# An MLP's up product as seven block products (Strassen) in three of its four groups, with the weight sums on GpSimd

## The chip, the cores and the metric

The kernel runs on one core of one Trainium2 chip. The metric is the device time of one launch in microseconds (us). A core has a matrix engine (TensorE, PE in the profile, with its weight loads as PEld), a vector engine (VectorE, DVE), a scalar engine (ScalarE, ACT), GpSimd (POOL) and SyncE (SP), which issues DMAs. Each engine runs its own instructions in order and waits for the others at semaphores.

## The reference

A trunk of two layers over 512 positions of 1024 channels, float32. Layer 0 mixes tokens with a gated DeltaNet, layer 1 with a Conformer convolution module. Each layer then cross-attends to a memory of 256 positions and applies the MLP that is changed here:

```python
def rms_norm(x, g):
    y = x * lax.rsqrt(jnp.mean(x * x, axis=-1, keepdims=True) + RMS_EPS)
    return y * g

def sq_relu_mlp(h, w_up, w_down):          # w_up (1024, 4096), w_down (4096, 1024)
    return jnp.square(jax.nn.relu(h @ w_up)) @ w_down

# in both layers
h = h + sq_relu_mlp(rms_norm(h, mlp_norm[layer]), mlp_w_up[layer], mlp_w_down[layer])
```

At the end stands a last RMS norm.

## The kernel before

Every float32 operand of a matmul is split into a high part (rounded to fp32r) and the low rest, and a product is three matmuls: high x high, low x high and high x low (`mm3`, L292 to L294). Activations lie with channels on partitions and 512 tokens along the row. `Norm.parts` makes the split of the MLP's input times its gain, without the root: `xs[k]` for k = 0 to 7. The factor 1/rms per token is computed by `Norm.stat` (a matmul with ones, a root, a reciprocal) and spread over partitions as `norm.rb`.

Weights come in a single stream, written out ahead in `order`, `loads` and `need`. `wload` issues one DMA of 128x1024 floats (512 KB) on SP's queue into a `raw` tile (six buffers); where blocks of the down product's weights must be added, `more` issues further DMAs on GpSimd's queue that add in flight, in part into `t` tiles (three buffers, tag `fs`). `wsplit` makes of a raw tile the high part `wh` on ScalarE (L251, a cast) and the low part `wl` on VectorE (L71, a subtraction); of `wh` and `wl` there are three buffers each. `wnext` hands out the next pair, issues loads some way ahead and splits up to three ahead. Which instruction stands where on its engine is settled when the program is built, by a scheduler with its own estimates; the text's order is not binding on it.

`mlp7(layer, norm, hres, ...)` works in four groups of 1024 of the 4096 hidden channels. In each group the up product makes eight tiles of 128 hidden channels x 512 tokens: eight times 24 matmuls with the weights as the stationary operand (128x128) and 512 tokens moving. `up_ev` takes a tile from PSUM: relu and the factor `norm.rb` in one VectorE step (`rl`, L77), the square on ScalarE (`u2`, L1100). `early` and `late` form differences and sums of halves of these tiles and split them into `ah`, `al`, `sh`, `sl`.

The down product `dn7` is already a Strassen scheme in Winograd's form: seven products of 512 x 256 x 512 instead of eight, in the order of `ORDER7` (in the last group `LAST7`), each on two units of weights and 24 matmuls of 512 columns. `into` adds a product to its accumulator `acc` on VectorE. Tokens 0 to 255 and 256 to 511 are the two row blocks. In the last group the weights' sums are made differently, and the results go on: in layer 0 through transposes (`outs`), in layer 1 through `final` to the output. In layer 1 `turn` puts the residual, transposed, into the accumulators during the first group.

## Time and profile before

| what | before |
|---|---|
| time, median of 3 runs | 1466.11 us (1464.77 to 1466.46) |
| profiled execution | 1465.14 us |
| its span, first to last instruction | 1463.4 us |
| granted TensorE clock | 0.998 |
| busy: PE, DVE, ACT, POOL | 1452.9, 1065.2, 771.2, 266.8 us |
| up product, 1536 matmuls of 512 columns | 351.3 us |
| down product, 1344 matmuls of 512 columns | 306.7 us |
| data moved by DMA | 201.82 MB, 138 GB/s on average |

Busy times are sums over one execution. Matmuls overlap in the pipeline, so a row's mean duration (about 390 ns at 512 columns) is longer than the spacing of their starts. In grouped rows stand: line, engine, operation, output tile <- inputs, shapes, count | busy us, mean ns of one | idle us of the engine just before them, and who ended it. A line can be that of a helper: L71 is every `tensor_tensor`, L77 every `scalar_tensor_tensor`.

### The profile page before, as it was taken

What the parts mean: (1) busy time and instruction counts of PE and PEld (TensorE: products, weight loads), DVE (VectorE), ACT (ScalarE), POOL (GpSimd) and SP (SyncE); (2) the same over time, 40 slices, a digit from 0 to 9 for tenths busy, and PEclk for the clock granted to TensorE, in tenths of its full rate; (3) what the DMA queues carried; (4) which work ended last, traced back from release to release, by engine and by line L of the source; (5) the groups of instructions that cost most, each with busy time, mean ns of one, the idle gap of its engine ahead of it and who ended that gap; (6) DMA issues with size and microseconds to landing.
All of it is one profiled execution on the core that took longest, in us unless ns stands there. A gap on an engine that the chain in (4) does not pass through costs nothing.

```text
span 1463.4 us, 19623 instructions
## 1 busy us (share of the span) xinstructions
PE 1452.9 (99%) x7298; PEld 1225.5 (84%) x7298; DVE 1065.2 (73%) x1615; ACT 771.2 (53%) x1326; POOL 266.8 (18%) x289
## 2 busy tenths in 40 slices
PE   9999999999999999999999999999999999999997
PEld 7888889988888888888888889988888888888886
DVE  6879889867646766767679899985555776767677
ACT  7766865655434464435355655564444544434354
POOL 1411310103113000010000486402113010000100
PEclk9999999999999999999999999999999999999999
DMA  8232124442213666584766624533214566575853
GB/s 283 84 115 73 59 87 158 132 143 87 72 44 108 166 165 179 140 199 136 202 159 215 185 82 162 179 129 100 72 51 127 139 169 177 135 210 131 229 144 87
DMA packets 62735, 201.82 MB, mean 138 GB/s; under 512 B 7728, under 2 KB 10032, under 8 KB 62640
## 3 DMA queue, kind: packets, MB, share of 16 engines
q1 hardware_dynamic: 52416, 164.39, 33.4%
q0 software_dynamic: 9792, 35.66, 14.3%
q8 instruction: 57, 0.93, 0.3%
q10 hardware_dynamic: 432, 0.52, 0.1%
q14 instruction: 38, 0.31, 0.1%
HBM read 197.66 MB, written 2.10 MB: 136 GB/s over the span
## 4 chain that ended last, share of the span: by engine, by line
PE 94%; DVE 3%; ACT 2%; DMA 1%; issue 0%; POOL 0%; SPq 0%; POOLq 0%; DVEq 0%
PE up L292 8%; PE up L294 8%; PE up L293 8%; PE dn L1130 6%; PE dn L1128 6%; PE dn L1129 6%; PE pw L294 3%; PE pw L292 3%; PE pw L293 3%; PE h L292 3%; PE h L293 3%; PE h L294 3%; PE xo L293 2%; PE xo L294 2%; PE q L292 2%; PE q L293 2%
## 5 line engine op out<-in xcount | busy, mean ns | idle before, releaser
L251 ACT CAST wh<-raw 128x1024 fp32r<-128x1024 f32 x259 | 271.6, 1051 | 358.7 <-issue 97.0
L71 DVE TENSOR_TENSOR wl<-raw,wh 128x1024 fp32r<-128x1024 f32 (+1 forms) x250 | 304.2, 1219 | 104.3 <-ACT wh L251 98.5
L292 PE MATMUL up<-xh,wh 128*128 128x512 f32 x512 | 199.7, 390 | 0.0
L294 PE MATMUL up<-xh,wl 128*128 128x512 f32 x512 | 199.3, 389 | 0.0
L293 PE MATMUL up<-xl,wh 128*128 128x512 f32 x512 | 199.2, 389 | 0.0
L294 PEld LDWEIGHTS up<-xh,wl 128*128 128x128 f32 x512 | 96.1, 188 | 20.1
L293 PEld LDWEIGHTS up<-xl,wh 128*128 128x128 f32 x512 | 96.2, 188 | 19.8
L292 PEld LDWEIGHTS up<-xh,wh 128*128 128x128 f32 x512 | 96.1, 188 | 19.7
L239 POOL DMA_DIRECT2D t<-w_dn x48 | 42.1, 915 | 354.2 <-DVE wl L71 239.0
L1128 PE MATMUL dn<-wh,ah 128*128 128x512 f32 x256 | 99.8, 390 | 0.0
L1130 PE MATMUL dn<-wl,ah 128*128 128x512 f32 x256 | 99.6, 389 | 0.0
L1129 PE MATMUL dn<-wh,al 128*128 128x512 f32 x256 | 99.6, 389 | 0.0
L77 DVE SCALAR_TENSOR_TENSOR rl<-up,rb 128x512 f32<-128x512 f32 x64 | 44.1, 690 | 58.4 <-PE up L294 58.4
L1358 DVE SCALAR_TENSOR_TENSOR ca<-x,prm,ca 128x512 f32<-128x512 f32 x112 | 82.3, 752 | 3.9 <-ACT ca L1355 1.5
L251 ACT CAST wh<-t 128x1024 fp32r<-128x1024 f32 x44 | 46.4, 1055 | 55.8 <-PE dn L1129 43.7
L71 DVE TENSOR_TENSOR wl<-t,wh 128x1024 fp32r<-128x1024 f32 x44 | 53.7, 1223 | 29.5 <-ACT wh L251 29.3
L292 PE MATMUL h<-xh,wh 128*128 128x512 f32 x184 | 73.7, 400 | 0.0
L71 POOL TENSOR_TENSOR sq<-sq,sq 128x512 f32<-128x512 f32 x28 | 45.4, 1621 | 148.3 <-ACT sq L385 134.2
L294 PE MATMUL h<-xh,wl 128*128 128x512 f32 x184 | 71.9, 391 | 0.0
L293 PE MATMUL h<-xl,wh 128*128 128x512 f32 x184 | 71.7, 390 | 0.0
L71 DVE TENSOR_TENSOR acc<-acc,dn 128x512 f32<-128x512 f32 x100 | 67.3, 682 | 1.2
L71 DVE TENSOR_TENSOR al<-u,ah 128x512 fp32r<-128x512 f32 x64 | 44.1, 688 | 21.4 <-ACT ah L331 21.4
(385 smaller groups left out, 3560.1 us busy)
## 6 DMA issues: line engine op xcount, KB each, us to landing
raw<-w_dn SPq DMA_DIRECT2D x68, 512.0 KB, 3.7
raw<-w_up SPq DMA_DIRECT2D x64, 512.0 KB, 4.3
t<-w_dn POOLq DMA_DIRECT2D x48, 512.0 KB, 6.0
raw<-w_pw SPq DMA_DIRECT2D x24, 512.0 KB, 3.7
raw<-w_dn POOLq DMA_DIRECT2D x20, 512.0 KB, 5.9
raw<-w_k SPq DMA_DIRECT2D x16, 512.0 KB, 3.6
raw<-w_vv SPq DMA_DIRECT2D x16, 512.0 KB, 4.1
t<-w_dn SPq DMA_DIRECT2D x16, 512.0 KB, 3.5
```

The source lines that it names most:

```text
L71: r = e.tensor_tensor(out=o, in0=a, in1=b, op=op)
L77: return dve.scalar_tensor_tensor(out=o, in0=a, scalar=s, in1=b, op0=op0, op1=op1)
L239: nc.gpsimd.dma_start(out=t, in_=a, accum_op=ALU.add)
L251: ins = [act.copy(h, raw)]
L292: pe.matmul(ps, wh, xh, start=first, stop=False)
L293: pe.matmul(ps, wh, xl, start=False, stop=False)
L294: pe.matmul(ps, wl, xh, start=False, stop=last)
L1128: pe.matmul(ps, xh, w[0][:, s], start=opens and k == 0, stop=False, skip_group_check=True)
L1129: pe.matmul(ps, xl, w[0][:, s], start=False, stop=False, skip_group_check=True)
L1130: pe.matmul(ps, xh, w[1][:, s], start=False, stop=k == 3, skip_group_check=True)
L1358: first["tap"] = dve.scalar_tensor_tensor(out=a, in0=src, scalar=w, in1=a, op0=ALU.mult, op1=ALU.add)
```

## The change

In groups two to four (g = 1 to 3; `PLAIN = 1`) of both layers the up product is also made of seven block products. A group has two halves `sg` of 512 hidden channels. In each half the 1024 x 512 weight block is cut into four blocks of 512 channels x 256 hidden channels, named 11, 12, 21, 22, and the input into halves by channels and by tokens. A block product is 24 matmuls with 256 tokens moving (L1329 to L1331 of the new file), into half of a PSUM bank per 128 hidden channels. Of the seven, products 0 and 2 go to one bank, 4 and 6 to another.

The four raw weight blocks are loaded as they are (four DMAs instead of four whole units, the same bytes). The sums T3 = 22 + 12, T1 = 12 + 11, T2 = 11 + T3 and T4 = 21 + T2 are made in place on GpSimd, in this order, once the plain blocks 11, 22 and 21 are split; each sum is then split as a unit of its own: seven casts and seven subtractions for a half instead of four. The sums on the input's side (`x_sums`) are made once a layer, during the second half of group one.

`fast` combines the products on VectorE (`uP`, `uQ`, `uW`), applies relu and square on ScalarE in two steps, forms the down product's operands (R3, R2, S1, S4) from whole blocks and splits all seven. Group one keeps the plain product, with the loops turned so that the first four input tiles are used up first.

The factor 1/rms is no longer applied to the hidden channels. relu(s x)^2 = s^2 relu(x)^2 for positive s, so the accumulators are multiplied by 1/rms^2 per token: `Norm.columns` computes rms^2, its reciprocal and the negative as columns by token; at the last group the accumulators so far are scaled on ScalarE, and the last group's products are scaled as they are added (`into`); `turn` multiplies the residual by rms^2 beforehand. The split of the sum of squares, the root, its reciprocal over 512 columns and the `rl` step are gone in the MLP.

In the built program the products of a first half stand on PE in the order of `UP7`. In a second half the third of them (12 by 21) stands behind the first matmuls of product 5, so that the order is 0, 1, 3, 4, 5 in part, 2, 5, 6, and some matmuls of the down product stand ahead of product 6's. The cast of T1 stands on ScalarE ahead of the copy of product 0 (`uP`).

```diff
+    def block_up(layer, g, sg, b):
+        a = int(b[0]) - 1
+        return w_up[layer, g * 4 + sg * 2 + int(b[1]) - 1][:, a * 1024:(a + 1) * 1024]
+
     def plan_mlp7(layer):
         for g in range(4):
-            for i in range(4):
-                plan(("up", layer, g * 4 + i), w_up[layer, g * 4 + i])
+            if g < PLAIN:
+                for i in range(4):
+                    plan(("up", layer, g * 4 + i), w_up[layer, g * 4 + i])
+            else:
+                for sg in range(2):
+                    n = len(loads)
+                    for b in UPLOAD:
+                        loads.append([block_up(layer, g, sg, b)])
+                    for u in range(7):
+                        order.append((("ups", layer, g, sg), u))
+                        need.append(n + (UPLOAD.index(UP7[u][1]) if u < 3 else 3))
...
+        if kind == "ups" and hf == 2:
+            t = TU
+            t["12"] = ws["raw"].pop(need[u] - 1)
+            for x, y in (("22", "12"), ("12", "11"), ("11", "22"), ("21", "11")):
+                tt(pool, t[x], t[x], t[y], ALU.add)
...
+    def combos_up(u, hf):
+        name = UP7[hf][1]
+        if hf < 3:
+            TU[name] = ws["raw"].pop(need[u])
+            return TU[name]
+        return TU[{"T1": "12", "T2": "11", "T4": "21", "T3": "22"}[name]]
...
+        def columns(self):
+            ps = psum("ssq")
+            for c in range(4):
+                pe.matmul(ps[:, c:c + 1], self.acc[:, c * P:(c + 1) * P], ones[:, 0:1], start=True, stop=True)
+            self.ms, self.r2, self.r2n = [keepc(4, s + str(self.cols)) for s in ("ms", "r2", "r2n")]
+            ts(dve, self.ms, ps[:, 0:4], 1.0 / 1024, ALU.mult, EPS, ALU.add)
+            dve.reciprocal(self.r2, self.ms)
+            ts(dve, self.r2n, self.r2, -1.0, ALU.mult)
...
-            act.copy(a, ps)
+            act.activation(a, ps, AF.Copy, scale=norm.ms[:, 2 * n + c:2 * n + c + 1])
...
-        def up_ev(ps):
-            t = slot(s="rl")
-            stt(t, ps, 0.0, norm.rb, ALU.max, ALU.mult)
-            u = slot(s="u2")
-            act.activation(u, t, AF.Square)
-            return u
+        def relu2(x, o):
+            act.activation(o, x, AF.Relu)
+            act.activation(o, o, AF.Square)
+            return o
...
+                elif g == 3 and key != ("p",):
+                    col = slice(2 * key[0] + c, 2 * key[0] + c + 1)
+                    dve.scalar_tensor_tensor(out=acc[k], in0=ps, scalar=(norm.r2 if op == ALU.add else norm.r2n)[:, col],
+                                             in1=acc[k], op0=ALU.mult, op1=ALU.add)
...
+        X = {"11": [[t[:, 0:256] for t in xs[k]] for k in range(4)],
+             "12": [[t[:, 0:256] for t in xs[4 + k]] for k in range(4)],
+             "22": [[t[:, 256:512] for t in xs[4 + k]] for k in range(4)], "R2": [], "S1": [], "R3": [], "S4": []}
+
+        def x_sums(k):
+            a, b = slot(s="xa"), slot(s="xb")
+            ga, gb = pc(norm.g, k), pc(norm.g, 4 + k)
+            tt(dve, b[:, 0:256], hres[k][:, 256:512], hres[k][:, 0:256], ALU.subtract)
+            act.activation(b[:, 0:256], b[:, 0:256], AF.Copy, scale=ga)
+            stt(a[:, 0:256], hres[4 + k][:, 256:512], gb, b[:, 0:256], ALU.mult, ALU.subtract)
+            stt(a[:, 256:512], hres[k][:, 0:256], ga, a[:, 0:256], ALU.mult, ALU.subtract)
+            stt(b[:, 256:512], hres[4 + k][:, 0:256], gb, a[:, 0:256], ALU.mult, ALU.subtract)
+            for t, names in ((a, ("R2", "S1")), (b, ("R3", "S4"))):
+                for name, p in zip(names, pair(split(t, "x"))):
+                    X[name].append(p)
+
+        def plain(g, sg, side):
+            us = []
+            for b in range(2):
+                pss = [psum("up") for _ in range(2)]
+                for a in range(2):
+                    w = wnext(("up", layer, g * 4 + sg * 2 + b), a)
+                    for j in range(2):
+                        for k in range(4):
+                            c = slice(k * 256 + j * P, k * 256 + j * P + P)
+                            mm3(pss[j], (w[0][:, c], w[1][:, c]), xs[4 * a + k], a == k == 0, a == 1 and k == 3)
+                            if (g, sg, b, a, j, k) == (0, 0, 0, 1, 0, 1):
+                                norm.columns()
+                    side(4 * sg + 2 * b + a)
+                us.append([relu2(ps, slot(s="u2")) for ps in pss])
+                for j in range(2):
+                    if b:
+                        late(ops[2 * sg + j], us[0][j], us[1][j])
+                    else:
+                        early(ops[2 * sg + j], us[0][j])
+
+        def fast(g, sg):
+            bank = {}
+
+            def product(u):
+                left, right, key, opens = UP7[u]
+                w = wnext(("ups", layer, g, sg), u)
+                if opens:
+                    bank[key] = psum("up")
+                for j in range(2):
+                    o = bank[key][:, j * 256:j * 256 + 256]
+                    for k in range(4):
+                        c = slice(k * 256 + j * P, k * 256 + j * P + P)
+                        xh, xl = X[left][k]
+                        pe.matmul(o, w[0][:, c], xh, start=opens and j == k == 0, stop=False, skip_group_check=True)
+                        pe.matmul(o, w[0][:, c], xl, start=False, stop=False, skip_group_check=True)
+                        pe.matmul(o, w[1][:, c], xh, start=False, stop=k == 3, skip_group_check=True)
+                return bank[key]
+
+            def give(name, x):
+                hl = split(x, "a")
+                for j in range(2):
+                    ops[2 * sg + j][name] = [t[:, j * 256:j * 256 + 256] for t in hl]

+            p, q, w, x11 = slot(s="uP"), slot(s="uQ"), slot(s="uW"), slot(s="u11")
+            act.copy(p, product(0))
+            f = product(1)
+            give("11", relu2(product(2), x11))
+            tt(dve, q, product(3), p, ALU.subtract)
+            tt(dve, w, product(4), q, ALU.add)
+            tt(dve, w, w, f, ALU.add)
+            give("12", relu2(w, w))
+            tt(dve, p, product(5), p, ALU.add)
+            b = product(6)
+            tt(dve, q, q, b, ALU.add)
+            tt(dve, p, p, b, ALU.subtract)
+            x22, x21 = relu2(q, q), relu2(p, p)
+            give("22", x22)
+            tt(dve, x21, x21, x11, ALU.subtract)
+            give("R3", x21)
+            tt(dve, x21, x22, x21, ALU.subtract)
+            give("R2", x21)
+            tt(dve, x11, x11, x21, ALU.subtract)
+            give("S1", x11)
+            tt(dve, w, w, x21, ALU.subtract)
+            give("S4", w)
...
+        def side(i):
+            if layer == 1:
+                if i:
+                    turn(i - 1)
+                if i == 7:
+                    turn(7)
+            if i > 3:
+                x_sums(i - 4)
...
+            if g == 3:
+                for n, m, c in [k for k in acc if len(k) == 3]:
+                    act.activation(acc[n, m, c], acc[n, m, c], AF.Copy, scale=norm.r2[:, 2 * n + c:2 * n + c + 1])
+            for sg in range(2):
+                if g < PLAIN:
+                    plain(g, sg, side if g == 0 else lambda i: None)
+                else:
+                    fast(g, sg)
...
+PLAIN = 1
+UPLOAD = ["11", "22", "12", "21"]
+UP7 = [("11", "11", "a", True), ("S4", "22", "f", True), ("12", "21", "a", False), ("S1", "T1", "c", True),
+       ("R2", "T2", "b", True), ("22", "T4", "e", True), ("R3", "T3", "b", False)]
```

More of the change, by code (lines that the diff above doesn't have):

```diff
@@ L246, in wsplit @@
         (kind, i, *j), hf = order[u]
-        raw = combos7(i, j[0], hf) if kind == "dn7" else ws["raw"].pop(need[u])
+        if kind == "dn7":
+            raw = combos7(i, j[0], hf)
+        elif kind == "ups":
+            raw = combos_up(u, hf)
+        else:
+            raw = ws["raw"].pop(need[u])
         h = wp.tile([P, 1024], F32R, tag="wh", name=nm("wh"), bufs=NW)
@@ L266, in wnext @@
         assert order[i] == (key, hf), (order[i], key, hf)
-        while ws["load"] <= need[min(i + NRAW + 1 + 2 * (order[i][0][0] in ("up", "dn7")), len(order) - 1)]:
+        while ws["load"] <= need[min(i + NRAW + 1 + 2 * (order[i][0][0] in ("up", "ups", "dn7")), len(order) - 1)]:
             wload()
@@ L272, in wnext @@
         return ws["hl"].pop(i)
+    TU = {}
+    def combos_up(u, hf):
[4 more added lines that the diff above has]
+        return TU[{"T1": "12", "T2": "11", "T4": "21", "T3": "22"}[name]]
     T7 = {}
@@ L368, in tile_trunk, with __init__ @@
     class Norm:
-        def __init__(self, gname):
-            self.g, self.acc, self.xs, self.n, self.side = gname, None, [], 0, None
+        def __init__(self, gname, cols=None):
+            self.g, self.acc, self.xs, self.n, self.side, self.cols = gname, None, [], 0, None, cols
         def add(self, t, h):
@@ L398, in square @@
                     tt(dve, self.acc, self.acc, self.side, ALU.add)
-                self.hl = split(self.acc, "sq")
+                if self.cols is None:
+                    self.hl = split(self.acc, "sq")
+        def columns(self):
[6 more added lines that the diff above has]
+            ts(dve, self.r2n, self.r2, -1.0, ALU.mult)
         def stat(self):
@@ L1234, in final @@
                 nc.sync.dma_start(out=yT[rows, gs], in_=y)
-        for g in range(4):
-            ops, us = [{} for _ in range(4)], []
-            for i in range(8):
-                w = wnext(("up", layer, g * 4 + i // 2), i % 2)
-                ps = psum("up")
-                proj(w, xs, ps, inside={1: norm.stat} if (g, i) == (0, 1) else None)
-                first.append(ps)
-                if (g, i) == (0, 0):
-                    continue
-                while first:
-                    us.append(up_ev(first.pop(0)))
-                    if len(us) % 2:
-                        early(ops[len(us) // 2], us[-1])
-                    else:
-                        late(ops[len(us) // 2 - 1], us[-2], us[-1])
-                if (layer, g) == (1, 0) and i > 1:
-                    turn(i - 2)
-            if (layer, g) == (1, 0):
-                turn(6)
-                turn(7)
+        X = {"11": [[t[:, 0:256] for t in xs[k]] for k in range(4)],
+             "12": [[t[:, 0:256] for t in xs[4 + k]] for k in range(4)],
+             "22": [[t[:, 256:512] for t in xs[4 + k]] for k in range(4)], "R2": [], "S1": [], "R3": [], "S4": []}
@@ new lines, in side @@
+        def side(i):
[6 more added lines that the diff above has]
+                x_sums(i - 4)
+        for g in range(4):
+            ops = [{} for _ in range(4)]
+            if g == 3:
[4 more added lines that the diff above has]
+                    plain(g, sg, side if g == 0 else lambda i: None)
+                else:
+                    fast(g, sg)
@@ L1687, in tile_trunk @@
         do_ev(m, do_mm(1, m))
-    n2 = Norm("mlp_norm0")
+    n2 = Norm("mlp_norm0", 0)
     h = xattn(0, n1, h, n2)
@@ L1693, in tile_trunk @@
     h = conformer(n3, h, n4, rest)
-    n5 = Norm("mlp_norm1")
+    n5 = Norm("mlp_norm1", 1)
     h = xattn(1, n4, h, n5)
@@ L1824, in _layout @@
     r["w_o"] = np.stack([_pack_a(np, i["xa_w_o"][j]) for j in range(2)])
-    halves = [8 * g + m for g in range(4) for m in (0, 4, 1, 5, 2, 6, 3, 7)]
-    r["w_up"] = np.stack([_pack_a(np, i["mlp_w_up"][j], halves) for j in range(2)])
+    r["w_up"] = f(np.stack(i["mlp_w_up"][:2]).reshape(2, 2, 4, 128, 4, 2, 2, 256).transpose(0, 4, 6, 5, 3, 1, 2, 7)
+                  .reshape(2, 16, 128, 2048))
     r["w_dn"] = np.stack([np.concatenate([_pack_b(np, i["mlp_w_down"][j][g * 1024:(g + 1) * 1024]) for g in range(4)]) for j in range(2)])
```

## The prediction

> **What bounds the kernel now.** I read the page's first block and chain, then PE's waits, then windows over one group of the MLP, then the timeline for the spacing of matmuls, last the grouped lines of the other engines.

> ```profile
> span 1463.4 us, 19623 instructions
> PE 1452.9 (99%) x7298; PEld 1225.5 (84%) x7298; DVE 1065.2 (73%) x1615; ACT 771.2 (53%) x1326; POOL 266.8 (18%) x289
> ...
> PE 94%; DVE 3%; ACT 2%; DMA 1%; issue 0%; POOL 0%; SPq 0%; POOLq 0%; DVEq 0%
> ```

> ```profile
> PE warm L130 <- POOL ones L127: 1.2, 1, 1.2
> PE h L1558 <- ACT xh L378: 1.0, 1, 1.0
> PE pw L294 <- POOL wl L71: 0.2, 1, 0.2
> PE dn L1130 <- DVE wl L71: 0.2, 1, 0.2
> ```

> TensorE is busy for 99% of the span and is 94% of the chain; its listed waits come to 2.6 us. So matmul time taken away is time won, as long as the other engines still deliver on time.

> ```profile
> core 0: us, PE busy (x) PEld busy (x) DVE busy (x) ACT busy (x) POOL busy (x), PEclk, DMA share, GB/s
> 555.50:599.00 43.50, 43.50 (x193) 36.05 (x192) 26.93 (x41) 19.45 (x29) 1.76 (x2) 1.00 0.58 158
> 599.00:637.10 38.10, 38.10 (x169) 31.54 (x168) 28.24 (x34) 16.76 (x19) 5.22 (x6) 1.00 0.70 178
> ```

> These are the second group of layer 0: its up product (192 matmuls, 43.5 us) and its down product (168 matmuls, 38.1 us). PE has no gap in either, and DVE is free for 16.6 and 9.9 us.

> **PE's side of the change.** A half group (96 matmuls of 512 columns) becomes seven products of 24 matmuls of 256 columns. Matmuls overlap, so their price is the spacing of starts. The K projection has the new form: 128x128 weights reloaded for each matmul, 256 columns.

> ```profile
> 502.93 0.39 PE L294 MATMUL up<-xh,wl 128*128 128x512 f32 x1
> ...
> 504.97 0.39 PE L294 MATMUL up<-xh,wl 128*128 128x512 f32 x1
> ```

> ```profile
> 241.83 0.28 PE L294 MATMUL K<-mh,wl 128*128 128x256 f32 x1
> ...
> 245.91 0.28 PE L292 MATMUL K<-mh,wh 128*128 128x256 f32 x1
> ```

> Nine starts in 2.04 us give 0.2267 us at 512 columns; 34 in 4.08 us give 0.120 at 256. A group's up product goes from 43.5 to 336 x 0.120 = 40.3 us. That is 3.2 us a group, 19 us over the six groups: all that PE can gain. A half lasts 20.2 us, one product 2.88.

> **The load on the others.** Durations:

> ```profile
> L71 DVE TENSOR_TENSOR wl<-raw,wh 128x1024 fp32r<-128x1024 f32 x246 | 302.5, 1232 | 99.6 <-ACT wh L251 98.5
> L71 DVE TENSOR_TENSOR acc<-acc,dn 128x512 f32<-128x512 f32 x100 | 67.3, 682 | 1.2
> L77 DVE SCALAR_TENSOR_TENSOR rl<-up,rb 128x512 f32<-128x512 f32 x64 | 44.1, 690 | 58.4 <-PE up L294 58.4
> L71 DVE TENSOR_TENSOR al<-u,ah 128x512 fp32r<-128x512 f32 x64 | 44.1, 688 | 21.4 <-ACT ah L331 21.4
> ```

> ```profile
> L251 ACT CAST wh<-raw 128x1024 fp32r<-128x1024 f32 x259 | 271.6, 1051 | 358.7 <-issue 97.0 <-PE dn L1129 82.4 <-PE up L293 77.8
> L1100 ACT ACTIVATE u<-rl 128x512 f32<-128x512 f32 x64 | 40.1, 626 | 10.4 <-DVE rl L77 10.2
> ```

> ```profile
> L71 POOL TENSOR_TENSOR sq<-sq,sq 128x512 f32<-128x512 f32 x28 | 45.4, 1621 | 148.3 <-ACT sq L385 134.2 <-issue 10.3 <-DVE wl L71 3.7
> L71 POOL TENSOR_TENSOR wl<-raw,wh 128x1024 fp32r<-128x1024 f32 x13 | 31.1, 2405 | 7.8 <-ACT wh L251 7.8
> ```

> Per half, DVE gets 7 weight subtractions (7 x 1.23 = 8.6), 7 operand subtractions (4.8), 4 differences out of SBUF (2.8) and 6 steps that read PSUM (4.1): 20.3 us in 20.2. ACT gets 7 casts (7.4) and 16 steps of about 0.62 (9.9): 17.3. POOL gets four in-place sums of 128x1024. Nothing in the trace is just that; wl on POOL (two operands, 1024 wide) is nearest, 2.40 each, 9.6 in all; at the sq row's pace it would be 2 x 1.62 = 3.24. I take 2.40.

> The sums do not run beside DVE freely:

> ```profile
> 1037.70 2.12 POOL L71 TENSOR_TENSOR pexp<-pexp,sm 128x512 f32<-128x512 f32 x1 [3.18 <-DVE sm L1004]
> ```

> ```profile
> 1037.70 1.22 DVE L71 TENSOR_TENSOR wl<-raw,wh 128x1024 fp32r<-128x1024 f32 x1
> 1038.84 1.53 DVE L71 TENSOR_TENSOR ql<-qf,qh 128x512 fp32r<-128x512 f32 x1
> ```

> ```profile
> L71 POOL TENSOR_TENSOR pexp<-pexp,sm x16: 1041/1042/2118, 381.4 to 1080.6; 128x512 f32<-128x512 f32 x16
> ```

> pexp takes 1.04 as a rule and 2.12 here: it stood still while wl ran, and ql (0.69 for its size in the al row) took 1.53, since it then stood behind pexp. So a DVE step with both operands in SBUF and a POOL step take turns. But not always:

> ```profile
> 836.68 4.76 POOL L71 TENSOR_TENSOR wl<-raw,wh 128x1024 fp32r<-128x1024 f32 x2
> ```

> ```profile
> 838.50 3.13 DVE L1358 SCALAR_TENSOR_TENSOR ca<-x,prm,ca 128x512 f32<-128x512 f32 x4
> ```

> Here four DVE steps (0.78 each) and two POOL steps (2.38 each) pass without loss. The changed steps are tensor_tensor, the kind that took turns, so I count them as exclusive.

> [...]

> **What becomes late.** There are three weight buffers, so a block's cast can begin when the product three places back has ended. Time runs from the start of a fast group.

> First half. POOL's first sum (T3) follows the subtraction of block 22, which ends about -0.2: it runs to 2.2. The subtraction of block 21 takes its turn, to 3.4, and the next sum (T1) runs to 5.8. In ACT's program order the cast of T1 (to 6.9) stands ahead of the copy of the first product out of its bank (0.6, to 7.5). The third product adds into that bank and is due at 2 x 2.88 = 5.8: **1.7 late**.

> Second half, from 20.2 + 1.7 = 21.9. In PE's program order T1 is here third, not fourth (block 21's product is put back behind T4's first matmuls), due at 27.7. Block 22's cast stands behind the activations of the first half, so T3 starts at about 22.7. With one operand subtraction before it and block 21's after it T1 runs from 26.7 to 29.1, its cast to 30.2: 2.5 late. Its subtraction is third in DVE's queue, and each of the two 0.69 steps ahead lets one more sum in: step to 29.8, T2 to 32.2, step to 32.9, T4 to 35.3, subtraction to 36.5. The product's third matmul, due at 30.5, waits 6.0 more: **8.5 late**.

> Down product. The operand steps left over (DVE free for 9.9 us, above) put weight subtractions one or two 0.69 steps back; between 0 and 5 us I take **1.7**, three such places.

> POOL's accumulating DMAs for the down blocks now stand behind the second half's last sum (35.3). With 0.9 for each issue (5.2 us for six in the window row) and these landings

> ```profile
> raw<-w_up SPq DMA_DIRECT2D x64, 512.0 KB, 4.3
> t<-w_dn POOLq DMA_DIRECT2D x48, 512.0 KB, 6.0
> ```

> the four are out by 39 and landed by 45. PE first needs one (T3) for the second down product, at 21.9 + 20.2 + 8.5 + 5.4 = 56.0: covered by 11 us, priced at nothing; beyond that cover POOL's delay would count one to one. On SP's queue the second half's block 12 waits for the buffer of T2 (subtracted at 5.8 + 2.4 + 1.2 + 2.4 + 1.2 = 13.0, by turns), lands 4.3 later, at 17.3, and is asked for at 22.7: covered by 5 us, nothing; the down loads behind it on that queue have still longer.

> A fast group: -3.2 + 1.7 + 8.5 + 1.7 = +8.7, so +52 over six.

> The rest. The left operands' sums in group one add per layer 4 x (2 x 0.69 + four half-width steps of about 0.48, which is 0.7 times 0.69) = 13.2 us of DVE and drop 8 x 0.69 = 5.5 (rl) and this:

> ```profile
> L408 DVE RECIPROCAL rb<-sd 128x512 f32<-128x512 f32 x5 | 16.8, 3353 | 2.9 <-ACT sd L406 2.9
> ```

> The net 4.3 us has room in the 26.5 free, but comes all in the group's second half: between 0 and 6 a layer, I take 2, +4. The factor 1/rms squared costs eight scalings (8 x 0.63) on ACT at the last group and otherwise replaces steps by their like (0.69 for 0.68): between 0 and 5 a layer, I take +3 in layer 0, where the last group ends in transposes that need all of ACT. In layer 1 the last group's down product starts with R3. Its second half's operand is due after 12 matmuls, 2.7 us behind the up product, and takes two PSUM steps, three activations, a difference, a cast and a subtraction, some in parallel: about 5.2; +2.5. Outside the MLP nothing changes.

> **Sum.** 52 + 4 + 5.5 = +61. The profiled execution took 1465.1 (span 1463.4 and 1.7 around it), 1.0 under the median of the runs. 1465.1 + 61 = **1526 us**. Its own range, with the turns lost in one half or some late steps spread, is 1500 to 1550.

> **Rivals.**
> A, faster: POOL and DVE deliver everything in time and PE's count decides: 1465.1 - 19 = 1446. It decides once T1 is split within 5.8 us of the start of a second half. For it: DVE is free for 26.5 us a group now. Against: even without turns T1 comes 1.9 us late there (B), and DVE's 20.3 us fill the half. Chance 0.06, parts of the gain included.
> B, no turns, as in the ca row. First half: T1 ends at -0.2 + 4.8 = 4.6, cast and copy at 6.3, 0.5 late. Second half, from 20.7: T3 from 21.5, T1 to 26.3, cast to 27.4 where 26.5 was due, subtraction to 28.6 where 27.6 was due: 1.9. With 1.7 for the down product +0.9 a group, +5 over six, +9.5 for the rest: 1480. Chance 0.26.
> C, the sums at the sq row's pace: 0.84 longer each; two lie on the first half's path, four on the second's: 5.1 us a group, +31: 1557. Chance 0.09.
> The forecast has 0.59.

> **How the numbers follow.** B reaches down to about 1474 (half of the down product's 6 x 1.7 less), C up to 1560; with these as the range, A and the tails beyond are left out, under 0.2. A measurement of this kernel tells 0.2% (3 us) from no change: A gives 0.05 faster; same 0.02, where A and B meet; the rest, 0.93, slower.

> **What would show it.** Right: up matmuls of 256 columns 0.12 apart; PE waiting in the up products on ACT wh and DVE wl, some 10 us a group, longest around 6; POOL sums of 2.4 stretched past 3, and DVE steps of 0.69 that take 2 to 3. Wrong: PE without waits over 1 us in the fast halves (A), sums at 2.4 and al at 0.69 side by side (B), or spacing far from 0.12, which would move everything.

## The result, and the profile after

The changed kernel takes 1545.46 us (median of three runs, 1543.41 to 1546.26) against 1466.11: a ratio of 1.0541, with a 95% interval of 1.0517 to 1.0565. Forecast were 1526 us and a range of 1474 to 1560. So the direction and the range held, and the size was 19 us short. The profiled execution has a span of 1543.7 us.

First the span and the engines on the page of the changed kernel:

```profile
span 1543.7 us, 21727 instructions
PE 1467.0 (95%) x8174; PEld 1264.0 (82%) x8174; DVE 1184.5 (77%) x1649; ACT 863.2 (56%) x1462; POOL 403.1 (26%) x337
```

PE has 876 matmuls more but is busy only 14 us longer; the rest of the 80 us that the span grew by is idle time: 77 us without a matmul instead of 10.5. PE's waits (us in total, how often, longest) say where:

```profile
PE up L1331 <- DVE wl L71: 30.1, 6, 5.0
PE up L1329 <- ACT wh L269: 7.9, 6, 1.3
PE up L1329 <- ACT uP L1340: 7.7, 6, 1.8
PE dn L1168 <- ACT wh L269: 5.3, 7, 1.9
PE dn L1170 <- DVE wl L71: 4.7, 8, 1.4
PE pw L326 <- POOL wl L71: 2.9, 1, 2.9
```

The first three come six times each, once in each of the six fast groups: 1.3 us for the copy of the first product (uP), 1.3 us for a cast and 5.0 us for a weight subtraction, both in the second half. Here are the stretches of group two of layer 0, that the prediction showed of before, and behind them the 5.6 us right after its wait of 5.0 us (columns: window, length, busy time of the engines with their counts, clock, DMA share, GB/s):

```profile
559.10:612.30 53.20, 45.73 (x333) 43.77 (x332) 41.19 (x35) 26.98 (x36) 25.86 (x12) 0.90 0.47 124
612.30:650.30 38.00, 37.27 (x174) 30.37 (x173) 32.08 (x41) 20.21 (x26) 3.65 (x5) 1.00 0.68 186
593.40:599.00 5.60, 5.60 (x26) 5.60 (x27) 4.17 (x6) 1.27 (x2) 0.57 (x1) 0.51 0.87 183
```

The two product stretches now overlap by some 20 matmuls, so the group is the better unit: 91.1 us (559.1 to 650.3) where it was 81.6. POOL has 25.9 us in the up product where it had 1.8. The last line is a thing that the prediction does not know: after the wait the granted clock is 0.51.

Why the subtraction is late is seen on the timelines of DVE and POOL in the second half of that group (start, duration, instruction):

```profile
581.02 0.68 DVE L71 TENSOR_TENSOR uQ<-uQ,up 128x512 f32<-128x512 f32 x1
581.62 0.68 DVE L71 TENSOR_TENSOR uP<-uP,up 128x512 f32<-128x512 f32 x1
582.21 2.26 DVE L71 TENSOR_TENSOR wl<-raw,wh 128x1024 fp32r<-128x1024 f32 x1
584.40 2.88 DVE L71 TENSOR_TENSOR uP<-uP,u 128x512 f32<-128x512 f32 x1
587.21 2.84 DVE L71 TENSOR_TENSOR al<-uQ,ah 128x512 fp32r<-128x512 f32 x1
589.97 3.36 DVE L71 TENSOR_TENSOR wl<-raw,wh 128x1024 fp32r<-128x1024 f32 x1
```

```profile
580.58 11.67 POOL L71 TENSOR_TENSOR raw<-raw,raw 128x1024 f32<-128x1024 f32 x4 [10.28 <-DVE wl L71]
```

POOL's four sums start at 580.58. The two DVE steps that take an operand out of PSUM (up) pass beside them at their usual 0.68. Each of the four that follow has both operands in SBUF, starts while a sum is running and takes 1.0 to 2.2 us more than its own 0.69 or 1.23: about what is left of that sum. These are the turns of the forecast. Of the 48 sums 12 ran undisturbed at 2.36 to 2.41 us, as priced; the others took 2.67 to 3.27.

### The profile page after: what moved, and what is told of

It is laid out like the page before. It is cut to its first block, busy times and chain, and to the rows that moved or that the text cites. A ratio compares the mean times of both kernels' runs of the same rounds, so it can differ in the third digit from the quotient of the medians.

```text
span 1543.7 us, 21727 instructions
## 1 busy us (share of the span) xinstructions
PE 1467.0 (95%) x8174; PEld 1264.0 (82%) x8174; DVE 1184.5 (77%) x1649; ACT 863.2 (56%) x1462; POOL 403.1 (26%) x337
## 5 line engine op out<-in xcount | busy, mean ns | idle before, releaser
L71 DVE TENSOR_TENSOR wl<-raw,wh 128x1024 fp32r<-128x1024 f32 (+1 forms) x286 | 391.3, 1371 | 151.5 <-ACT wh L269 123.4
L1331 PE MATMUL up<-xh,wl 128*128 128x256 f32 x672 | 196.8, 293 | 30.1 <-DVE wl L71 30.1
L1329 PE MATMUL up<-xh,wh 128*128 128x256 f32 x672 | 196.9, 293 | 15.6 <-ACT wh L269 7.9
L1330 PE MATMUL up<-xl,wh 128*128 128x256 f32 x672 | 195.2, 290 | 0.0
L71 POOL TENSOR_TENSOR raw<-raw,raw 128x1024 f32<-128x1024 f32 x48 | 136.3, 2839 | 139.0 <-DVE wl L71 136.2
L1168 PE MATMUL dn<-wh,ah 128*128 128x512 f32 x400 | 156.5, 398 | 6.2 <-ACT wh L269 5.3
L1331 PEld LDWEIGHTS up<-xh,wl 128*128 128x128 f32 x672 | 134.8, 201 | 31.3 <-DVE wl L71 31.3
L1169 PE MATMUL dn<-wh,al 128*128 128x512 f32 x400 | 156.6, 392 | 1.6 <-DVE al L71 1.6
L1329 PEld LDWEIGHTS up<-xh,wh 128*128 128x128 f32 x672 | 134.8, 201 | 18.5 <-ACT wh L269 9.1
L1170 PEld LDWEIGHTS dn<-wl,ah 128*128 128x128 f32 x400 | 75.5, 189 | 27.3 <-DVE wl L71 12.1
L1168 PEld LDWEIGHTS dn<-wh,ah 128*128 128x128 f32 x400 | 74.7, 189 | 27.7 <-ACT wh L269 8.8
L1169 PEld LDWEIGHTS dn<-wh,al 128*128 128x128 f32 x400 | 75.4, 188 | 18.0 <-DVE al L71 2.6
L71 POOL TENSOR_TENSOR sq<-sq,sq 128x512 f32<-128x512 f32 x28 | 45.5, 1625 | 150.4 <-ACT sq L417 136.2
## 6 DMA issues: line engine op xcount, KB each, us to landing
raw<-w_dn SPq DMA_DIRECT2D x68, 512.0 KB, 6.0
raw<-w_up SPq DMA_DIRECT2D x64, 512.0 KB, 3.6
t<-w_dn POOLq DMA_DIRECT2D x48, 512.0 KB, 6.2
raw<-w_pw SPq DMA_DIRECT2D x24, 512.0 KB, 3.6
raw<-w_dn POOLq DMA_DIRECT2D x20, 512.0 KB, 8.5
raw<-w_k SPq DMA_DIRECT2D x16, 512.0 KB, 3.6
raw<-w_vv SPq DMA_DIRECT2D x16, 512.0 KB, 4.0
t<-w_dn SPq DMA_DIRECT2D x16, 512.0 KB, 4.5
```

The source lines that it names most:

```text
L71: r = e.tensor_tensor(out=o, in0=a, in1=b, op=op)
L1168: pe.matmul(ps, xh, w[0][:, s], start=opens and k == 0, stop=False, skip_group_check=True)
L1169: pe.matmul(ps, xl, w[0][:, s], start=False, stop=False, skip_group_check=True)
L1170: pe.matmul(ps, xh, w[1][:, s], start=False, stop=k == 3, skip_group_check=True)
L1329: pe.matmul(o, w[0][:, c], xh, start=opens and j == k == 0, stop=False, skip_group_check=True)
L1330: pe.matmul(o, w[0][:, c], xl, start=False, stop=False, skip_group_check=True)
```

## The experiments

All times are medians, each with its ratio to the kernel before on the same chip. They go in order of what they tell.

**The weight sums left out.**

```diff
             t["12"] = ws["raw"].pop(need[u] - 1)
-            for x, y in (("22", "12"), ("12", "11"), ("11", "22"), ("21", "11")):
-                tt(pool, t[x], t[x], t[y], ALU.add)
```

> Leaves out the four weight sums of each fast half on GpSimd; the last four products multiply the raw blocks instead, so the output is another one. Everything else is as in the changed kernel (1545 us). Theory (the sums take turns with VectorE's steps, and the product that needs T1 comes late): VectorE's steps out of SBUF go back to 0.69 and 1.23 us, PE's waits on DVE wl (5.0 a group) and on ACT uP (1.3) go, the clock stays at 1.00, a fast group takes 78.4 to 80 us instead of 90 to 91; with the extra that the changed kernel has in the last groups, in group one and behind the MLP (some 20 us) the time is 1465 to 1480 us. Rival (VectorE has 20.3 us of work in a half of 20.2, so it is late by its own load): the waits on DVE wl stay near 5 us a group and the time stays above 1530.

Measured: 1477.55 us, 1.0078 (1.0063 to 1.0093). The same group, in one window:

```profile
558.60:639.20 80.60, 79.82 (x505) 71.59 (x504) 61.39 (x74) 47.09 (x62) 6.08 (x7) 1.00 0.59 165
```

PE's waits for wl and uP in the up products are gone, the clock is 1.00, and the group is 1.0 us shorter than before the change, though not within the 78.4 to 80 us expected. DVE is busy for 61.4 of 80.6 us and keeps up: its own load is not the cause. Two of its steps from the second half, which took 2.88 and 2.84 us beside the sums:

```profile
582.01 0.69 DVE L71 TENSOR_TENSOR uP<-uP,u 128x512 f32<-128x512 f32 x1 [0.63 <-ACT uP L1138]
582.62 0.68 DVE L71 TENSOR_TENSOR al<-uQ,ah 128x512 fp32r<-128x512 f32 x1
```

The sums cost 68 of the 79 us.

**Sums that nobody reads, first try.** The sums go into a scratch tile, in two halves each:

```diff
+                for s in (slice(0, 512), slice(512, 1024)):
+                    tt(pool, scr, t[x][:, s], t[y][:, s], ALU.add)
```

> The same sums from the same blocks on GpSimd (each as two of half the width), but into a scratch tile that nobody reads; the last four products multiply the raw blocks, so the output is another one. What is left of the sums is only that they run beside VectorE. Theory (turns and lateness both count): VectorE's 0.69 us steps are stretched past 1.2 on average again, the wait for T1 is short, and the time lies between the run without sums and the changed kernel, 1490 to 1525 us. Rival (no turns, only the chain sum, cast, subtraction is late): VectorE's steps at 0.69, and the time is that of the run without sums within 5 us. Second rival (turns alone): 1535 us or more.

Measured: 1549.45 us, 1.0571 (1.0547 to 1.0595). This looks like the second rival, but the run does not show it. PE waits elsewhere, and what ScalarE waits for in turn says why (PE's wait, then ACT's):

```profile
PE dn L1170 <- ACT wh L269: 33.8, 12, 5.9
```

```profile
ACT wh L269 <- DMA t<-w_dn: 66.7, 11, 12.1
```

Sums into a scratch tile need not wait for the splits of their blocks, so they stand elsewhere in POOL's queue, and the accumulating transfers of the down blocks behind them come late: PE waits 4.8 to 5.9 us near the end of five of the eight down products. In the up products, where the turns are, a second half takes 19.0 us, from its start to the first matmul of the down product, instead of the 17.5 without sums. For the turns at their place in the changed kernel the run is inconclusive. It shows something else: POOL's queue, for which the prediction counted 11 us of cover, costs as soon as that cover is gone.

**Sums that nobody reads, second try.** In place and behind the same splits as in the changed kernel, so that POOL's queue keeps its order:

```diff
-            for x, y in (("22", "12"), ("12", "11"), ("11", "22"), ("21", "11")):
+            for x, y in (("22", "12"), ("12", "11"), ("11", "22"), ("22", "11")):
...
-        return TU[{"T1": "12", "T2": "11", "T4": "21", "T3": "22"}[name]]
+        return TU["21"]
```

> The four sums run on GpSimd in place as in the changed kernel, each behind the same splits, but nobody reads them: the last four products all multiply block 21 (so the output is another one), and the fourth sum goes into block 22 instead of 21. Unlike in the scratch run the order on GpSimd's queue is that of the changed kernel. It keeps the turns and takes away the wait for a sum. Theory (the turns stretch VectorE's steps, and half of the loss is that, half the chain sum, cast, subtraction): between the run without sums (1477.6) and the changed kernel (1545.5), 1495 to 1525 us, with waits on DVE wl of 2 to 4 us a group. Rival (only the chain counts): 1485 us or less. Second rival (only the turns count): 1535 us or more.

Measured: 1539.44 us, 1.0501 (1.0487 to 1.0516): the second rival, not what I expected. PE's longest waits, and the same four steps of DVE with the sums beside them:

```profile
PE up L1331 <- DVE wl L71: 42.7, 6, 7.3
```

```profile
581.05 2.25 DVE L71 TENSOR_TENSOR wl<-raw,wh 128x1024 fp32r<-128x1024 f32 x1
583.22 2.89 DVE L71 TENSOR_TENSOR uP<-uP,u 128x512 f32<-128x512 f32 x1
586.04 2.83 DVE L71 TENSOR_TENSOR al<-uQ,ah 128x512 fp32r<-128x512 f32 x1
588.79 3.35 DVE L71 TENSOR_TENSOR wl<-raw,wh 128x1024 fp32r<-128x1024 f32 x1
```

```profile
579.42 11.65 POOL L71 TENSOR_TENSOR raw<-raw,raw 128x1024 f32<-128x1024 f32 x4 [8.34 <-DVE wl L71]
```

To 0.01 us the durations of the changed kernel. No product waits for a sum any more, and still 62 of the 68 us stay: PE waits once for 6.9 to 7.3 us instead of for 1.3, 1.3 and 5.0. In the four middle groups, where little else differs, a group takes 89.3 to 91.1 us against 90.2 to 91.1 in the changed kernel and 80.6 without sums. So waiting for a sum as such costs some 6 us in the whole kernel, and the price is that DVE's queue stands still. That holds for this place: a second half takes 26.1 to 28.0 us here, but 19.0 to 20.9 in the scratch run, where nobody reads the sums either but the two sets of group two start some 12 and 27 us earlier in relation to the group. (Some of the 62 us lie in the last group of layer 0, where PE waits another 5.2 us behind a block that POOL's queue landed late; of that more below.)

**T1 first.**

```diff
-            for x, y in (("22", "12"), ("12", "11"), ("11", "22"), ("21", "11")):
-                tt(pool, t[x], t[x], t[y], ALU.add)
+            if hf == 0:
+                tt(pool, t["12"], t["12"], t["11"], ALU.add)
+            elif hf == 1:
+                tt(pool, t["22"], t["22"], t["12"], ALU.add)
+            else:
+                tt(pool, t["21"], t["21"], t["22"], ALU.add)
+                tt(pool, t["11"], t["22"], t["11"], ALU.subtract)
```

> Same sums on GpSimd, in another order: T1 (12 + 11) first, right behind the split of block 11, then T2 = 22 + T1, T4 = 21 + T2, and T3 = T2 - 11 last; the blocks are loaded in the order 11, 12, 22, 21. The order of the work on TensorE, ScalarE and VectorE is unchanged. Theory (T1 is late since it is the second of the sums and each step of VectorE ahead of its subtraction lets one more sum in): the wait on DVE wl falls from 5.0 to 1 to 2.5 us a group, the clock's falls behind it go, and the time is 1500 to 1522 us, with the VectorE steps still stretched. Rival (the turns as such fill the half, and it doesn't matter which sum is first): 1537 us or more.

Measured: 1533.49 us, 1.0468 (1.0447 to 1.0489), between the two expectations. The first half has no wait left (20.2 us) and neither has the cast, but the long one stays at 4.5 to 5.1 us. Two steps of DVE stand ahead of T1's subtraction as before, and each lets a sum in, now T2's and T4's. The middle groups gain little (88.5 to 91.3 us); most of the 12 us won lie in the last groups, 94.8 instead of 102.8 and 90.5 instead of 94.6. The two steps and T1's subtraction:

```profile
582.65 2.88 DVE L71 TENSOR_TENSOR uP<-uP,u 128x512 f32<-128x512 f32 x1
585.46 3.30 DVE L71 TENSOR_TENSOR al<-uQ,ah 128x512 fp32r<-128x512 f32 x1
588.69 1.21 DVE L71 TENSOR_TENSOR wl<-raw,wh 128x1024 fp32r<-128x1024 f32 x1
```

**The sums in quarters**, so that a turn is short, in the order of the run above:

```diff
+        for c in range(0, 1024, 256):
+            s = slice(c, c + 256)
+            tt(pool, TU[o][:, s], TU[a][:, s], TU[b][:, s], op)
```

> As the run with T1 first (1533.5 us), and each sum on GpSimd is cut into four instructions of 256 columns. GpSimd's whole time is no shorter. Theory (a VectorE step waits for the GpSimd instruction that is running, so the two steps ahead of T1's subtraction wait for 0.6 us each instead of a whole sum): the wait on DVE wl falls from 4.5 to 5.1 us a group to 1 to 2.5, the steps al<-uQ and uP<-uP,u take 0.9 to 1.4 instead of 1.8 to 2.0, and the time is 1500 to 1518 us. Rival (only the whole 9.6 us of GpSimd in a half count): 1528 to 1540.

Measured: 1543.88 us, 1.0532 (1.0513 to 1.0551). My theory falls, and the rival's range is missed by 4 us too. The turns are shorter, as the theory says, but there are more of them:

```profile
L71 DVE TENSOR_TENSOR uP<-uP,u 128x512 f32<-128x512 f32 x12 | 10.1, 838 | 3.3 <-ACT uP L1151 3.3
L71 POOL TENSOR_TENSOR raw<-raw,raw 128x256 f32<-128x256 f32 x192 | 204.6, 1112 | 153.0 <-DMA raw<-w_up 78.1 <-DVE wl L71 70.5 <-issue 4.3
```

A quarter takes 1.11 us, a sum 4.4, and PE's waits for wl and wh in the up products (22.4 and 7.7 us) come to no less than the long one before. By the prediction's rows DVE's steps with two SBUF operands in a half (8.6 + 4.8 + 2.8 = 16.2 us) and POOL's 9.6 make 25.8 us if they take turns, in a half of 20.2. At this place neither the order nor the grain that was tried gets round that. But the count alone does not settle the time: the scratch run has the same steps and sums, and its second halves lose 1.5 us, with the sums at another place.

**The sums on DVE**, at the same place, and then in the order of the run with T1 first, with a square root added in group one (its reason stands further below). The edit of the first:

```diff
-                tt(pool, t[x], t[x], t[y], ALU.add)
+                tt(dve, t[x], t[x], t[y], ALU.add)
```

> The four sums of each fast half run on VectorE instead of GpSimd, at the same place in its program. VectorE then has 20.3 + 4 x 1.23 = 25.2 us in a half of 20.2, but nothing takes turns. Theory (turns and the late T1 are the price, not VectorE's count): the steps of 0.69 keep that length, T1's wait shrinks from 5.0 to under 2.5 us, and with work put off into the down product (where VectorE has 9.9 us free) the time is 1490 to 1525. Rival (VectorE's load is what counts): later than the changed kernel, 1550 to 1600 us.

> The sums on VectorE as in the earlier run (1510.8 us), but each as soon as its blocks are split, T1 first, then T2, T4 and T3; and the square root in group one. Theory (order counts on one engine too): the two waits of 1.8 us a group shrink to under 1, no fall of the clock in the second halves, 2.6 us less for the table: 1485 to 1500 us. Rival (VectorE has 25.2 us of work in 20.2, the order within does not matter): 1504 to 1511.

Measured: 1510.77 us, 1.0308 (1.0293 to 1.0324), and 1502.74 us, 1.0249 (1.0232 to 1.0266). The first is as its theory said. The second misses its theory's range by 2.7 us and the rival's by 1.3: the two waits shrank to 0.7 and 0.8 us, as the theory said, but the clock still fell in two of the six second halves. Sums and waits of the first, then waits of the second:

```profile
L71 DVE TENSOR_TENSOR raw<-raw,raw 128x1024 f32<-128x1024 f32 x48 | 58.6, 1220 | 0.2
```

```profile
PE up L1329 <- ACT wh L269: 11.0, 6, 1.8
PE up L1331 <- DVE wl L71: 10.8, 6, 1.8
```

```profile
PE up L1341 <- DVE wl L71: 4.8, 6, 0.8
PE up L1339 <- ACT wh L269: 4.2, 6, 0.7
```

A sum takes 1.22 us on DVE, 2.4 on POOL, and nobody takes turns (the first run's al steps take 0.69 on average). "More work on the busier engine" is 35 us better than "work on the idle engine". The count of the half does not explain this (25.2 us on DVE alone against 25.8 by turns); what stands in DVE's queue in the second half fits better. Unread sums on POOL lengthen the four steps shown above by 7.5 us together, and PE waits 6.9 to 7.3; four sums on DVE take 4.9, and PE waits 3.6. In the second run the order counts: 8 us, of which the root can explain little (0.9 us or so, below). A middle group then takes 83.1 to 83.2 us (84.6 in one case with a fall of the clock).

**What is left without weight sums.** Plain products in all groups, with and without the left operands' sums, and the factor with a square root in group one:

```diff
-PLAIN = 1
+PLAIN = 4
```

```diff
-            if i > 3:
-                x_sums(i - 4)
```

```diff
             ts(dve, self.r2n, self.r2, -1.0, ALU.mult)
+            act.activation(small(1), eps_ln, AF.Sqrt)
```

> All four groups of each layer take the plain up product; the factor 1/rms squared still goes to the output and the left operands' sums are still made in group one, with nobody reading them. PE's work is that of the kernel before. Theory (the extra in group one, 3.0 and 0.9 us, most of that in the last groups, and the 5.3 us behind the first MLP belong to the moved factor and to these sums, not to the fast products): group one of layer 0 at 85 us, the stretch behind the MLP at 327 to 328 instead of 322.4, the last group of layer 0 at 87 to 89, and the time is 1474 to 1482 us. Rival (they belong to the fast products): 1466 to 1470.

> Plain up products in all groups and no sums of left operands: of the change only the factor 1/rms squared, taken to the output, is left. The run with these sums took 1477.7. Theory (the sums' 13 us of VectorE in the second half of group one are what group one loses, 3.0 and 0.9 us; the 3.7 us behind the MLP and the 1.7 us at the end come with the factor): 1471.5 to 1475 us. Rival (group one loses its time to the columns of the norm and to the squares, not to the sums): 1476 to 1479.

Measured: 1477.73 us, 1.0082 (1.0067 to 1.0097), with the left sums; 1475.11 us, 1.0061 (1.0045 to 1.0076), with the factor alone, 0.1 above its range. The intervals overlap, but in the traces the left sums are about the 3 us that were expected: without them group one takes 82.6 us instead of 85.1 in layer 0, 86.4 instead of 86.8 in layer 1. The last group of layer 0 takes 85.4 us in both, not the expected 87 to 89; so most of its extra belongs to the fast products and their sums. The factor costs 9 us by itself, most of it in the stretch behind the first MLP, where the change edits next to nothing (at its end the split of a sum of squares is dropped). The stretch before, and with the factor alone:

```profile
802.70:1125.20 322.50, 322.17 (x1714) 276.56 (x1713) 240.98 (x340) 169.65 (x289) 120.10 (x80) 1.00 0.37 119
```

```profile
805.90:1133.60 327.70, 324.18 (x1712) 277.65 (x1711) 242.85 (x341) 171.50 (x290) 120.46 (x80) 0.99 0.35 117
```

2.9 us of it are one wait for a weight subtraction on POOL (the last of the changed kernel's PE waits above; 0.2 before), to which a fall of the clock of 3.41 us was added in some runs (327.7 us with one, 326.1 without); the rest are small shifts of the outputs' transposes and the norm. Which step upstream sets them off was not settled. A square root was one suspect:

> The changed kernel with one more activation: a square root of a constant on ScalarE in group one of each layer, where the kernel before had its own square root. Theory (ScalarE's function table for the root was loaded there, and the change put the load of 1.28 us on the path of the norm behind the first MLP and of the outputs at the end): 2.6 us less, 1541.5 to 1544.5 us. Rival (the load is hidden): 1545 to 1546.5.

> The factor alone, as in the run before it, with the square root of a constant in group one of each layer. Theory (each of the two table loads of 1.28 us stood on the path): 2.6 us less than the factor alone, between 1.5 and 3.5. Rival (the place of the load does not matter): within 1 us of it.

Before, ScalarE loaded its function table for the root in group one; with the factor alone it does so at the norm behind the MLP:

```profile
479.95 1.28 ACT L406 ACT_TABLE_LOAD   x1
```

```profile
824.11 1.28 ACT L448 ACT_TABLE_LOAD   x1
```

Measured: 1543.87 us, 1.0535 (1.0519 to 1.0551), for the changed kernel with the root, where 1.0541 was without it; 1474.23 us, 1.0056 (1.0044 to 1.0069), for the factor with it, 0.9 under the factor alone. The first lies in its theory's range and the second in its rival's. Both intervals overlap with those without the root, so a gain isn't shown. In the traces of the pair with the factor alone the load is gone from the norm, yet the stretch takes 327.7 us in both; only the tail behind the last matmul is 1.2 us shorter (8.0 instead of 9.2). Of the two loads at most the one at the end lay on the path.

Here is the ladder, with the lengths of the groups from the starts of their first matmuls (stretch: from the end of the first MLP's matmuls to the second MLP; tail: behind the last matmul; us):

| | before | factor | + left sums | + fast products | + sums, unread | changed |
|---|---|---|---|---|---|---|
| median | 1466.1 | 1475.1 | 1477.7 | 1477.6 | 1539.4 | 1545.5 |
| layer 0: group 1 | 82.1 | 82.6 | 85.1 | 85.2 | 85.2 | 85.2 |
| groups 2, 3 | 81.6, 81.6 | 81.6, 81.6 | 81.6, 81.6 | 80.6, 80.6 | 89.4, 91.1 | 91.1, 90.2 |
| group 4 | 84.0 | 85.4 | 85.4 | 88.3 | 102.2 | 102.8 |
| stretch | 322.4 | 327.7 | 326.1 | 327.8 | 326.2 | 327.8 |
| layer 1: group 1 | 85.8 | 86.4 | 86.8 | 86.7 | 86.8 | 86.7 |
| groups 2, 3 | 81.6, 81.6 | 81.6, 81.6 | 81.6, 81.6 | 80.6, 80.6 | 89.8, 89.3 | 90.2, 91.0 |
| group 4 | 81.8 | 82.2 | 82.2 | 83.3 | 93.6 | 94.6 |
| tail | 7.4 | 9.2 | 9.2 | 9.9 | 9.9 | 10.2 |

The fourth column is the floor: with the weight sums for nothing the kernel would still be slower than before. The fast products win 4 us in the four middle groups and lose as much in the last ones. So no placing of the sums alone gets below the kernel before, and none was tried beyond those above. Fast products with the factor left at the hidden channels were not tried either.

## Why the prediction was nearly right, step by step

**PE's gain** (3.2 us a group). Right: without sums an up half takes 20.2 us, as 168 x 0.120 says. With the down product's waits 1.0 a group is left.

**The turns.** Right, and they are the bulk: 61 us forecast for the late products in six groups (1.7 + 8.5 each), 68 measured for the sums as a whole (falls of the clock and a late transfer included, see below). But one of the rows on which their chance was weighed was misread. I took `ca<-x,prm,ca` for a step with two SBUF operands that runs beside POOL without loss, and gave rival B 0.26 for it. Its accumulator `ca` is a PSUM bank (the code allocates it with psum), as `up` is in the two undisturbed steps above. So the row said nothing on steps with two SBUF operands. In the changed kernel's trace all 42 such steps of DVE that started during a sum were stretched, by 0.84 to 2.20 us over their 0.69 or 1.23, which is within 0.15 us of what was left of the sum; the 17 that started there with one operand in PSUM (up or dn) kept their 0.68 to 0.69. B deserved much less.

**First half, 1.7 late.** Measured 1.1 to 1.8, by the way described: the wait is on uP's copy.

**Second half, 2.5 + 6.0 late.** Measured 1.3 + 5.0, by the same steps in the same order. What the description put in front, that T1 is asked for too early, is not the cause, though: where nobody reads T1 the wait is as long, and T1 first shortens it by half a us at most.

**Down product, 1.7.** Some 2 in the regular groups: without sums 80.6 us stand against 40.3 + 38.1 = 78.4, with 0.2 of it in the up product.

**The step that was left out: the clock.** A regular fast group lost 8.6 to 9.5 us, and 8.7 was forecast, but the parts are others. The waits in the up product came to 7.4 to 7.6 us instead of 10.2, and behind the 5.0 us wait TensorE ran at half its clock. Two matmuls of 256 columns from that place:

```profile
593.76 0.41 PE L1329 MATMUL up<-xh,wh 128*128 128x256 f32 x1
593.98 0.41 PE L1330 MATMUL up<-xl,wh 128*128 128x256 f32 x1
```

They start 0.21 apart instead of 0.12. The window of 5.6 us at a clock of 0.51, above, holds 26 matmuls that take 3.1 at full speed: 2.5 us lost. In the other groups the fall ends 3.0 to 5.7 us behind the wait, which is 1.3 to 2.6 us each and 12 in all. The prediction set this at nothing: it let a wait cost its own length. In the middle groups that error and the waits counted too long cancelled, so the 8.7 was hit partly by luck.

**The terms that were mis-sized.** They make most of the 19 us that were missing. The last groups: group four of layer 0 is 11.7 us longer than group two of it where it was 2.4 longer before, 9.3 of extra against the 3 forecast. By the ladder 1.4 come with the factor (the scalings, all that I had counted), 3.9 with the fast products (without sums PE waits 1.0 and 0.6 us there for a block of operands, ah and al, and a fall of the clock follows) and 4.0 with the sums, see the next paragraph. In layer 1 the extra over the regular groups is 3.8 (from 0.2 to some 4.0) where I had 2.5. And "outside the MLP nothing changes" is wrong: 5.4 us behind the first MLP and 2.8 at the tail. The left operands' sums (4) came to 3.

**The prices set at nothing.** No wait of PE ends with a transfer directly, and in five of the six fast groups those in the down product are the ones of the run without sums. In the last group of layer 0 POOL's accumulating transfers were not free. Behind the four sums they are issued some 16 us later in the group than without sums; the cast of a block waits for the landing (7.3 us) and PE for the cast:

```profile
786.99 1.16 POOL L252 DMA_DIRECT2D raw<-w_dn  x1
798.41 1.04 ACT L269 CAST wh<-raw 128x1024 fp32r<-128x1024 f32 x1 [7.28 <-DMA raw<-w_dn]
799.51 0.50 PE L1168 MATMUL dn<-wh,ah 128*128 128x512 f32 x1 [1.94 <-ACT wh L269]
```

That block landed at 798.3. PE waits 3.2 us in three places there, two blocks late in the same way, and the clock falls at 800.3 for 3.41 us. The cover of 11 us was counted for a regular group and does not hold for the last one, where the weights' sums are made differently. With unread sums a wait behind such a block takes 5.2 us, and the scratch run brings such waits to five other groups.

**Rivals.** A and B are out: PE does wait, and the steps with two SBUF operands did take turns with the sums (2.07 to 3.36 us instead of 0.69 or 1.23). C's price was wrong too: an undisturbed sum takes 2.4 us, as assumed, not 3.24.

## What to carry to other kernels

An idle engine was not free capacity here (the sums cost 68 us): before moving work to GpSimd, look which of VectorE's steps with two SBUF operands it will meet and what waits behind them, and count both engines' time together; if that doesn't fit into the stretch, the same work on VectorE (1.22 us a sum here instead of 2.4, and 35 us less in all) may be cheaper, or an earlier place for it. Count, too, what a wait of TensorE brings behind it through the clock (some 12 us here). To tell contention from lateness, keep the work where it is and let nobody read it, and check that the queues keep their order. When a row is to show that two things don't collide, look up in which memory each operand lies.
